# Hybrid streaming encoder step on one core: W_out loaded by parts, two output tiles under the last attention, scratch kept by token tile

## The chip, the cores and the metric

The kernel runs on one core of a Trainium2 chip. The metric is the device time of one execution in microseconds. The engines are named as in the profile: PE (TensorE, matmuls), DVE (VectorE), ACT (ScalarE), POOL (GpSimd) and SP (SyncE, whose queue issues all DMAs of this kernel).

## The reference, cut to what matters

One layer over 1024 prompt tokens and 8 x 16 sample tokens, 1152 in all, 1024 features wide. One projection gives the columns of three attention groups and a gate; the gated, concatenated attention outputs go through W_out, a residual and a LayerNorm.

```
h = x @ w_in                         # 3584 columns: A q,k,v; B q,k,v; M q; gate (1024)
o_a = band attention, 4 heads x 64, own chunk of 64 and 8 before, bias by distance
o_b = differential attention, 4 heads (2 maps of 64, values 128), rotary, then RMS norm and gain
o_m = attention of 4 heads x 64 into 256 memory tokens, keys and values from mem @ w_mem_kv
y = (concat(o_a, o_b, o_m) * silu(gate)) @ w_out
out = LayerNorm(ALPHA * x + y)       # and the new keys and values of each group are returned
```

The prompt attends to itself; each sample stream attends to its cache and its own 16 new tokens.

## The kernel before

All is fp32, and precision is kept by splitting: each operand becomes a rounded high part (fp32r) and the rest as a low part, and a product is three matmuls (high x high, high x low, low x high). A split is an ACT copy and a DVE or POOL subtraction (`split_half`, L122, for the input weights).

Tokens go in 3 chunks of 384 (`CH`) for the projections and in 9 tiles of 128 for the output. x lies split in SBUF all through the projections, in pool `xp`: `x{h,l}{c}`, 3 chunks of 8 feature rows. W_in has 28 blocks of 128 columns; a block is 3 chunks x 8 feature rows x 3 matmuls (`step`, L139). Two weight blocks are held (`wst`, tags `whi`, `wlo`), and `load_next` (L127) loads and splits the next one when a block begins, in the order of the list `order` (L113 to L119).

Heads go in pairs, as 8 units in the order `ORD` = M0, B0 to B3, A0, A1, M1. A unit has a key block, a value block, its attention over 8 query tiles, and the stages of its sample part. The attention (`attention_m`, `_b`, `_a`) is a list of steps with weights; `merge` (L943) mixes it with a filler list, the projections that don't depend on it: the unit's values, `NG[i]` gate blocks and the next unit's queries. Sample stages (`sample`, L774) are spread over later fillers (`with_stages`). Within this written order the planner places each instruction on its engine by a model of when its inputs are ready, so work may stand far ahead of where it is written.

A query tile's scores are two matmuls (L440, L441); DVE takes the row maximum (L588, L753, or with bias L701), ACT the exponential with its row sum, PE transposes it (L453), ACT and DVE split it (L456, L457), PE multiplies with the values (L627, L666). For A and M0 the sums are not divided out there: they are kept in `u.r`, and `finish` (L496) turns them into factors, written to the scratch `rscr`. For M1 (`slot == 7`) the rows are divided at once (`normalise`, L521), and its output stays in SBUF (`u.out`). For B the factor also holds the RMS norm.

Scratch in DRAM lies by column block: `oscr` [7, 128, 1152] takes the outputs of the seven other units, `gscr` [8, 128, 1152] the eight gates (L430), `rscr` [2, 8, 9, 128] the factors.

In the before kernel the last unit, M1, has two gate blocks as its filler. Behind it comes the output part. `mixed(t)` (L1032) loads for tile t the gates (L1037), the outputs (L1039) and, by six broadcasts over 64 partitions, the factors of A, B and M (L1044); it multiplies (L1048, L1058, L1062) and splits (L1054, L1055). W_out is loaded (L1149) and split (L1150, L1151) into the room of x, once the last gate has read x. Tiles 0 and 1 run k by k together, in four PSUM accumulators of two pools (`ps_s`, `ps_p`); tiles 2 to 8 run one after another in pieces of 512 columns (`piece`, L1097), with M1's sample stages between them. `add` (L1089) adds the residual (`xn`, loaded at L1076) and takes statistics, `norm` (L1103) normalises and stores. For tile 8 the second piece is cut in two of 256 columns, and the norm is shared between engines.

Cached keys and values of the samples go through one buffer (`sp`, tag `kc`). LayerNorm's scales are loaded behind W_out, `ln_g` into the buffer `tab0`, `ln_b` into `ka0`, which also holds the keys `u.ka[0]` of the attention.

## Time and profile before

| | |
|---|---|
| three runs | 698.63 us median (697.14 to 699.35) |
| profiled execution | 695.99 us, span 694.2 us |
| mean granted PE clock | 0.981 |
| busy: PE, DVE, ACT, POOL | 667.8, 467.1, 352.8, 210.3 us |
| DMA queue | 79.95 MB, 35.7% of 16 engines' span |

PE stands as busy over 96% of the span, but its matmuls are pipelined and their ends are modelled, so the share doesn't say how fast they follow each other; the distance from one start to the next does. `PEclk` is the share of the full clock (2.4 GHz) that was granted in a stretch; half speed is 1.2 GHz. In groups of instructions, "idle" is the time the engine stood before them and `<-` what released it. DMA times run from issue to landing.

### The profile page before, as it was taken

Reading aid. Unit: us, or ns where it says so; the run is one execution under the profiler, and the core shown is the slowest. Engines: PE = TensorE matmul, PEld = TensorE weight load, DVE = VectorE, ACT = ScalarE, POOL = GpSimd, SP = SyncE. Lnnn points to the kernel's source line nnn. Section 1 sums busy time; section 2 is a strip of 40 time slices with the busy share of each in tenths; the row PEclk is TensorE's granted clock in tenths of the full one; section 3 lists DMA queues with packets and bytes.
Section 4 is the critical chain, followed back from the end, with each engine's and each line's share of the span. In section 5 each row is a group of like instructions: output and inputs, shape, how many; then the busy total and the mean of one; then the engine's idle time right before and its main releaser. Section 6 shows DMA issues by size and latency. Waiting matters only on the chain.

```text
span 694.2 us, 12200 instructions
## 1 busy us (share of the span) xinstructions
PE 667.8 (96%) x4309; PEld 617.9 (89%) x4309; DVE 467.1 (67%) x1119; ACT 352.8 (51%) x917; POOL 210.3 (30%) x250
## 2 busy tenths in 40 slices
PE   8899999999999999999999999999999979798995
PEld 7799899999899999999999999999999958576784
DVE  4968756887687766896767256663566785788744
ACT  6748635575555645565557455574575762111000
POOL 7653213532343333432423121211110322223102
PEclk9999999999999999999999999999999979899998
DMA  8751432121212221152202121322232389897311
GB/s 280 255 197 58 143 116 74 50 94 70 66 50 83 83 89 61 50 172 92 75 24 90 69 73 51 108 73 96 92 108 88 122 243 280 237 272 222 117 66 61
DMA packets 68785, 80.72 MB, mean 116 GB/s; under 512 B 10210, under 2 KB 49780, under 8 KB 68724
## 3 DMA queue, kind: packets, MB, share of 16 engines
q1 hardware_dynamic: 68724, 79.95, 35.7%
q8 instruction: 34, 0.56, 0.3%
q14 instruction: 27, 0.22, 0.1%
HBM read 59.46 MB, written 20.46 MB: 115 GB/s over the span
## 4 chain that ended last, share of the span: by engine, by line
PE 82%; DMA 7%; DVE 5%; ACT 2%; issue 2%; SPq 2%; POOL 0%; POOLq 0%; DVEq 0%
PE pp L140 16%; PE pp L142 16%; PE pp L141 16%; PE ps L1087 5%; PE pt L453 5%; PE po L627 4%; PE ps L440 4%; PE ps L441 4%; PE pp L1087 4%; PE po L666 3%; DMA p<-gates 2%; PE pt L878 1%; SPq L1044 1%; PE ps L794 1%; DVE xl L198 1%
## 5 line engine op out<-in xcount | busy, mean ns | idle before, releaser
L140 PE MATMUL pp<-xh,whi 128*128 128x384 f32 x672 | 230.7, 344 | 1.1 <-DVE t L429 0.8
L141 PE MATMUL pp<-xl,whi 128*128 128x384 f32 x672 | 228.8, 341 | 2.4 <-DVE xl L198 1.8
L142 PE MATMUL pp<-xh,wlo 128*128 128x384 f32 x672 | 229.1, 341 | 0.0
L141 PEld LDWEIGHTS pp<-xl,whi 128*128 128x128 f32 x672 | 126.5, 188 | 6.0 <-DVE xl L198 2.4
L140 PEld LDWEIGHTS pp<-xh,whi 128*128 128x128 f32 x672 | 126.5, 188 | 4.6 <-DVE t L429 1.5
L142 PEld LDWEIGHTS pp<-xh,wlo 128*128 128x128 f32 x672 | 126.4, 188 | 1.8 <-issue 0.2
L125 POOL TENSOR_TENSOR wlo<-wraw,whi 128x512 fp32r<-128x512 f32 x54 | 73.0, 1372 | 144.0 <-ACT whi L124 142.0
L593 ACT ACTIVATE p<-ps,nm 128x512 f32<-128x512 f32 (+3 forms) x96 | 55.2, 580 | 56.5 <-DVE nm L590 37.7
L440 PE MATMUL ps<-ka,qa 128*128 128x512 f32 (+4 forms) x176 | 58.1, 337 | 1.2 <-ACT p L754 1.2
L441 PE MATMUL ps<-kl,qa 128*128 128x512 f32 (+4 forms) x176 | 56.8, 326 | 0.0
L453 PE MATMUL pt<-ident,p 128*128 128x128 f32 x332 | 55.0, 278 | 1.6 <-DVE rs L485 1.0
L588 DVE TENSOR_REDUCE nm<-ps 128x1 f32<-128x512 f32 (+3 forms) x96 | 50.9, 546 | 4.4 <-PE ps L441 2.8
L453 PEld LDWEIGHTS pt<-ident,p 128*128 128x128 f32 x332 | 40.3, 143 | 4.3 <-DVE rs L485 1.4
L457 DVE TENSOR_TENSOR ptl<-pt,pth 128x512 fp32r<-128x512 f32 x56 | 38.1, 684 | 5.7 <-ACT pth L456 5.4
L456 ACT CAST pth<-pt 128x512 fp32r<-128x512 f32 x56 | 32.4, 586 | 17.8 <-PE pt L453 11.0
L1054 ACT CAST whi<-p 128x1024 fp32r<-128x1024 f32 (+2 forms) x9 | 8.6, 954 | 62.6 <-PE pp L1087 39.1
L124 ACT CAST whi<-wraw 128x512 fp32r<-128x512 f32 x54 | 30.9, 620 | 9.9 <-PE pp L141 7.4
L440 PEld LDWEIGHTS ps<-ka,qa 128*128 128x128 f32 x176 | 33.1, 189 | 1.8 <-ACT p L754 1.4
L627 PE MATMUL po<-pth,va 128*128 128x256 f32 (+1 forms) x160 | 34.1, 284 | 0.0
L461 DVE TENSOR_TENSOR ptl<-pt,pth 128x256 fp32r<-128x256 f32 (+1 forms) x72 | 25.3, 352 | 13.1 <-ACT pth L460 12.7
L441 PEld LDWEIGHTS ps<-kl,qa 128*128 128x128 f32 x176 | 33.2, 189 | 0.2
L519 POOL COPY r<-rs 128x1 f32<-128x1 f32 x32 | 6.5, 203 | 88.4 <-DVE rs L597 44.7
(241 smaller groups left out, 1335.9 us busy)
## 6 DMA issues: line engine op xcount, KB each, us to landing
wraw<-in_win SPq DMA_DIRECT2D x54, 256.0 KB, 2.8
xr<-in_xT SPq DMA_DIRECT2D x12, 384.0 KB, 7.8
gates<-t SPq DMA_DIRECT2D x24, 192.0 KB, 1.9
qa<-in_xn SPq DMA_DIRECT2D x9, 512.0 KB, 6.1
out_y<-qa SPq DMA_DIRECT2D x16, 256.0 KB, 3.0
mixed<-od SPq DMA_DIRECT2D x28, 128.0 KB, 2.4
p<-mixed SPq DMA_DIRECT2D x8, 448.0 KB, 6.5
p<-gates SPq DMA_DIRECT2D x7, 512.0 KB
```

The costliest lines, as they stand in the source:

```text
L125: eng.tensor_tensor(out=lo[:, h], in0=raw, in1=f(hi[:, h]), op=ALU.subtract)
L140: nc.tensor.matmul(ps, lhsT=w[0][:, k], rhs=xh_[:, k], start=(k == 0), stop=False)
L141: nc.tensor.matmul(ps, lhsT=w[0][:, k], rhs=xl_[:, k], start=False, stop=False)
L142: nc.tensor.matmul(ps, lhsT=w[1][:, k], rhs=xh_[:, k], start=False, stop=(k == KT - 1))
L440: nc.tensor.matmul(ps, lhsT=u.qa[h][:, qs], rhs=u.ka[h][:, k0 : k0 + n], start=True, stop=False)
L441: nc.tensor.matmul(ps, lhsT=u.qa[h][:, qs], rhs=kl[h][:, k0 : k0 + n], start=False, stop=True)
L453: nc.tensor.transpose(pt[:, t, q * P : (q + 1) * P], p[q][:, cols[t][q] : cols[t][q] + P], ident)
L457: nc.vector.tensor_tensor(out=lo, in0=pt, in1=f(hi), op=ALU.subtract)
L588: nc.vector.tensor_reduce(out=nm[:, m, c : c + 1], in_=ps[c][:, : b - a], axis=AX.X, op=ALU.max, negate=True)
L593: nc.scalar.activation(e[:, a:b], ps[c][:, : b - a], AF.Exp, bias=nm[:, m, 0:1], accum_out=rs[:, m, c : c + 1])
L627: nc.tensor.matmul(out, lhsT=a, rhs=b, start=(g == 0 and x == 0), stop=(g == j and x == len(mm) - 1))
L1087: nc.tensor.matmul(y, lhsT=a[:, k], rhs=b[k][:, s], start=(k == 0 and x == 0), stop=(k == KT - 1 and x == 2))
```

## The change

- `NG` becomes [1, 1, 1, 1, 1, 1, 2, 0]: one gate runs at the start beside M0's query, chunk by chunk, and the last two run under A1 instead of M1. The second weight block is loaded ahead of x's chunks 1 and 2.
- Under A1, behind the queries of M1, the two gates run by chunk, and behind each chunk `load_wout(c)` loads up to three rows of W_out into that chunk's part of x.
- M1's filler is `out_steps(0)` and `out_steps(1)`: inputs, products by k, add and norm of the output tiles 0 and 1, both in `ps_p`. Row k = 7 (M1's own output) is handed out only when M1's pair of query tiles is closed; `merge` takes no more filler while it isn't.
- `normalise` divides all rows of A and M, samples too; `factors` and its scratch go, and `rscr` holds B's factors alone, in one broadcast per tile.
- The scratch lies by token tile: `oscr` [9, 128, 7, 128], `gscr` [9, 128, 8, 128]. A tile's load is one run per partition (3.5 or 4 KB instead of 7 or 8 runs of 512 bytes); a gate's store is three runs of 512 bytes per partition instead of one of 1.5 KB.
- The sample's matmuls get a priority, and M1's sample takes its key and value buffers from the pool `pp` (six buffers).

`add`, `products`, `piece` and `norm` are moved up unchanged but for the names of the scales.

```diff
-NG = [0, 1, 1, 1, 1, 1, 1, 2]
+NG = [1, 1, 1, 1, 1, 1, 2, 0]
...
-    oscr = dram.tile([7, P, NTOK], F32, tag="mixed")
-    gscr = dram.tile([8, P, NTOK], F32, tag="gates")
+    oscr = dram.tile([9, P, 7, P], F32, tag="mixed")
+    gscr = dram.tile([9, P, 8, P], F32, tag="gates")
...
-    rscr = dram.tile([2, 8, 9, P], F32, tag="rstd")
+    rscr = dram.tile([9, 4, P], F32, tag="rstd")
...
             for blk in range(4):
                 mem_part(blk)
+            load_next(ep)
             load_x(1)
             load_x(2)
-            load_next()
...
-            nc.sync.dma_start(gscr[slot, :, c * CH : (c + 1) * CH], t)
+            nc.sync.dma_start(
+                gscr[3 * c : 3 * c + 3, :, slot].rearrange("t p c -> p t c"), t.rearrange("p (t c) -> p t c", c=P))
...
-                nc.scalar.activation(
-                    e[:, :n], e[:, :n], AF.Exp, bias=nm, scale=-1.0, accum_out=u.r[:, 9 * h + i : 9 * h + i + 1])
+                rs = small.tile([P, 1], F32, tag="rs")
+                nc.scalar.activation(e[:, :n], e[:, :n], AF.Exp, bias=nm, scale=-1.0, accum_out=rs)
+                normalise(e[:, :n], rs, False)
...
-                    if u.slot == 7:
-                        normalise(e[:, h], u.r[:, 9 * h + i : 9 * h + i + 1], h == 1)
+                    rs = small.tile([P, 1], F32, tag="rs")
+                    nc.scalar.activation(e[:, h], ps, AF.Exp, bias=nm[:, h : h + 1], accum_out=rs)
+                    normalise(e[:, h], rs, h == 1)
...
-                               lambda: close_pair(u, st["po"], j))
+                               lambda: (close_pair(u, st["po"], j), closed.append(j)))
...
-            with tc.manual_schedule(engines={PE}):
+            with tc.high_priority(offset=SP_), tc.manual_schedule(engines={PE}):
...
+        def last(tag, shape):
+            return pp.tile(shape, F32, tag="p") if u.slot == 7 else sp.tile(shape, F32, tag=tag)
...
             while fill and done_f < lead + (total_f - lead) * rate * done_m / total_m:
-                c, g = fill.pop(0)
+                if len(fill[0]) == 3 and not fill[0][2]():
+                    break
+                c, g = fill.pop(0)[:2]
...
+    def mixed(t):
+        ts_ = slice(t * P, (t + 1) * P)
+        gt = sp.tile([P, KT, P], F32, tag="kc") if t == 0 else pp.tile([P, KT, P], F32, tag="p")
+        nc.sync.dma_start(gt, gscr[t])
+        mx = op_.tile([P, 7, P], F32, tag="tab0") if t == 0 else pp.tile([P, 7, P], F32, tag="p")
+        nc.sync.dma_start(mx, oscr[t])
+        rs = tmp.tile([P, 4, P], F32, tag="rs", bufs=2)
+        nc.sync.dma_start(rs, rscr[t].rearrange("(o k) c -> o k c", o=1).broadcast_to([P, 4, P]))
+        nc.vector.scalar_tensor_tensor(
+            out=mx[:, 2:6], in0=mx[:, 2:6], scalar=subg, in1=rs, op0=ALU.mult, op1=ALU.mult)
+        mh, ml = [wst.tile([P, KT, P], F32R, tag=tag) for tag in ("whi", "wlo")]
...
+        (nc.vector if t < 2 else nc.gpsimd).tensor_tensor(out=gt[:, 0:7], in0=mx, in1=gt[:, 0:7], op=ALU.mult)
+
+        def last():
+            nc.vector.tensor_tensor(out=gt[:, 7], in0=units[7].out[:, ts_], in1=gt[:, 7], op=ALU.mult)
+            parts(slice(7, 8) if t < 2 else slice(0, 8))
+
+        if t < 2:
+            parts(slice(0, 7))
+        else:
+            last()
+        return mh, ml, last
...
+    def load_wout(c):
+        room = [xp.tile([P, 3, 1024], F32R, tag=f"x{i}{c}") for i in "hl"]
+        for k in range(3 * c, min(3 * c + 3, KT)):
+            hi, lo = woh[k], wol[k] = [r[:, k - 3 * c] for r in room]
+            for n in range(2):
+                s = slice(512 * n, 512 * n + 512)
+                raw = wst.tile([P, 512], F32, tag="wraw")
+                nc.sync.dma_start(raw, d["wout"][k, :, s])
+                nc.scalar.copy(hi[:, s], raw)
+                (nc.gpsimd if n else nc.vector).tensor_tensor(out=lo[:, s], in0=raw, in1=f(hi[:, s]), op=ALU.subtract)
+
+    def out_steps(t, u):
+        st = {}
+        def go(k):
+            if k == 0:
+                start(t)
+                if t == 0:
+                    scales()
+                st["y"] = [ps_p.tile([P, 512], F32, tag="pp") for _ in CUTS]
+            if k == KT - 1:
+                outs[t].m[2]()
+            for cut, y in zip(CUTS, st["y"]):
+                products(t, cut, y, k)
+            if k == KT - 1:
+                residual(t)
+                for n, (cut, y) in enumerate(zip(CUTS, st["y"])):
+                    add(t, n, cut, y)
+                norm(t)
+        steps = [(1.4, lambda k=k: go(k)) for k in range(KT - 1)]
+        return steps + [(1.4, lambda: go(KT - 1), lambda: t // 2 in u.closed)]
+
+    def scales():
+        for w, tag in (("ln_g", "tab0"), ("ln_b", "ka0")):
+            norms.append(op_.tile([P, 1024], F32, tag=tag))
+            nc.sync.dma_start(norms[-1], d[w].broadcast_to([P, 1024]))
...
             if i == 6:
-                stages = sample_of(u)[:-1]
+                for c in range(3):
+                    for g in gs:
+                        fill += g[c]
+                    fill.append((0.0, lambda c=c: load_wout(c)))
+                stages = sample_of(u)
...
-            fill = more
+            fill = out_steps(0, u) + out_steps(1, u)
```

## Rows read from the trace of the kernel before

**Rows 1.** Stretches: busy us of PE, PEld, DVE, ACT, POOL; clock; DMA; GB/s

```profile
480.00:540.00 60.00, 60.00 (x441) 58.58 (x440) 36.21 (x108) 36.08 (x97) 6.00 (x8) 1.00 0.26 87
540.00:560.00 20.00, 16.46 (x108) 15.19 (x107) 15.12 (x41) 15.30 (x42) 5.73 (x4) 0.97 0.45 145
560.00:580.00 20.00, 18.83 (x85) 15.52 (x84) 18.16 (x35) 11.78 (x22) 6.20 (x4) 0.77 0.93 283
580.00:600.00 20.00, 15.90 (x82) 12.24 (x80) 8.81 (x18) 2.68 (x3) 4.21 (x2) 0.91 0.85 231
600.00:620.00 20.00, 20.00 (x92) 15.48 (x92) 17.23 (x28) 2.07 (x5) 6.64 (x4) 0.92 0.98 277
620.00:640.00 20.00, 17.39 (x106) 13.47 (x104) 16.60 (x33) 2.76 (x6) 6.17 (x4) 1.00 0.79 233
640.00:660.00 20.00, 19.92 (x109) 15.99 (x110) 15.59 (x27) 1.31 (x2) 3.93 (x3) 0.91 0.36 132
660.00:680.00 20.00, 20.00 (x87) 16.09 (x86) 11.21 (x19) 1.05 (x1) 1.83 (x2) 1.00 0.15 56
```

**Rows 2.** The chain that ended last, its last matmuls: start us, us, what

```profile
652.64 5.62 PE ps L1087 x24
...
680.75 5.65 PE pp L1087 x48
```

**Rows 3.** Stretch 540 to 694, L1087 alone: busy us of PE, PEld; clock; DMA

```profile
540.00:694.00 154.00, 109.11 (x456) 85.32 (x456) 0.92 0.60 183
```

**Rows 4.** Waits of PE, 500 to 694: us in total, times, longest

```profile
PE pt L878 <- DMA kc<-in_cmv: 2.7, 1, 2.7
PE ps L794 <- DVE qa L1094: 2.5, 1, 2.5
```

**Rows 5.** Timeline of PE: start us, us, instruction, idle before and its releaser

```profile
549.65 0.22 PE L666 MATMUL po<-ptl,va 128*64 128x128 f32 x1
...
582.66 0.28 PE L666 MATMUL po<-pth,va 128*128 128x256 f32 x1
...
598.29 1.22 PE L1087 MATMUL pp<-xh,whi 128*128 128x512 f32 x2 [1.60 <-DVE qa L1094]
```

**Rows 6.** Groups of splits on ACT, POOL and DVE: busy us, mean ns, idle

```profile
L124 ACT CAST whi<-wraw 128x512 fp32r<-128x512 f32 x54 | 30.9, 620 | 9.9 <-PE pp L141 7.4 <-issue 2.1 <-DMA wraw<-in_win 0.3
L125 POOL TENSOR_TENSOR wlo<-wraw,whi 128x512 fp32r<-128x512 f32 x54 | 73.0, 1372 | 144.0 <-ACT whi L124 142.0 <-DMA rs<-rstd 1.3 <-POOL qa L155 0.7
L1151 DVE TENSOR_TENSOR xl<-wraw,xh 128x512 fp32r<-128x512 f32 x2 | 2.1, 1052 | 0.4 <-ACT xh L1150 0.4
```

**Rows 7.** DMA issues: count, KB, median us to landing; then line L1044's

```profile
wraw<-in_win SPq DMA_DIRECT2D x54, 256.0 KB, 2.8
qa<-in_xn SPq DMA_DIRECT2D x9, 512.0 KB, 6.1
p<-mixed SPq DMA_DIRECT2D x8, 448.0 KB, 6.5
...
L1044 SPq DMA_DIRECT2D rs<-rstd x54: 512/599/3516, 396.3 to 633.9; - x54
```

**Rows 8.** Groups of DVE

```profile
L523 DVE RECIPROCAL ra<-ra 128x1 f32<-128x1 f32 x18 | 2.6, 152 | 0.9 <-ACT p L754 0.8
L528 DVE TENSOR_SCALAR p<-p,ra 128x256 f32<-128x256 f32 x8 | 3.1, 383 | 0.3
L921 DVE TENSOR_SCALAR tab<-tab 128x1280 f32<-128x1280 f32 x2 | 1.7, 849 | 0.3 <-DMA tab<-in_abias 0.3
L1094 DVE SCALAR_TENSOR_TENSOR qa<-qa,ps 128x512 f32<-128x512 f32 x9 | 6.0, 681 | 1.4 <-PE ps L1087 1.1
```

**Rows 9.** The first 30 us, and PE's largest hole in them

```profile
0.00:30.00 30.00, 25.12 (x154) 22.39 (x154) 19.26 (x23) 19.99 (x34) 22.93 (x28) 1.00 0.79 269
...
27.47 0.44 PE L141 MATMUL pp<-xl,whi 128*128 128x384 f32 x1 [1.64 <-DVE xl L198]
```

**Rows 10.** Timeline of SP's queue, W_out's first load

```profile
515.66 0.33 SPq L1149 DMA_DIRECT2D wraw<-in_wout  x1
```

More of the change, by code (lines that the diff above doesn't have):

```diff
@@ L24 @@
 BIG = 1e30
+SP_ = 100
 HP = 300
@@ L116, in hybrid_step @@
         order += [b + idx for b in base[kind][1:]]
-        order += [20 + next(gates) for _ in range(NG[i])]
+        late = [20 + next(gates) for _ in range(NG[i])]
+        if i != 6:
+            order += late
         if i < 7:
             order.append(base[names[i + 1][0]][0] + names[i + 1][1])
+        if i == 6:
+            order += late
     loaded = {}
@@ L496, in finish @@
     def finish(u):
-        src = u.ms if u.kind == "B" else u.r
-        if u.kind == "B":
-            factors_b(u)
-        else:
-            factors(u)
-        n = src.shape[-1]
-        pt = ps_t.tile([n, P], F32, tag="pt")
-        nc.tensor.transpose(pt, src, ident)
-        row = tmp.tile([n, P], F32, tag="od128", bufs=1)
+        factors_b(u)
+        pt = ps_t.tile([9, P], F32, tag="pt")
+        nc.tensor.transpose(pt, u.ms, ident)
+        row = tmp.tile([9, P], F32, tag="od128", bufs=1)
         nc.scalar.copy(row, pt)
-        for h in range(2):
-            nc.sync.dma_start(rscr[h, u.slot], row[n - 9 : n] if h else row[0:9])
+        nc.sync.dma_start(rscr[:, u.idx], row)
     def combine(u, ex, rs, n, t):
@@ L668, in attention_a @@
     def attention_a(u, need):
-        u.r = small.tile([P, 18], F32, tag="ra", bufs=2)
         blocks = []
@@ L739, in attention_m @@
             u.out = op_.tile([P, NTOK], F32, tag="tab1")
-        u.r = small.tile([P, 18], F32, tag="ra", bufs=2)
+        u.closed = closed = []
         blocks = []
@@ L907, in sample @@
             return stages
[L908 removed]
+        return stages
     def load_mem(u):
@@ L935, in emit @@
     def emit(items):
-        for _, fn in items:
-            fn()
+        for x in items:
+            x[1]()
     def stage():
@@ L945, in merge @@
         total_m = sum(w for w, _ in main)
-        total_f = sum(w for w, _ in fill)
+        total_f = sum(x[0] for x in fill)
         done_m = done_f = 0.0
@@ L1152, in hybrid_step @@
-    residual(0)
-    residual(1)
-    lng = op_.tile([P, 1024], F32, tag="tab0")
-    lnb = op_.tile([P, 1024], F32, tag="ka0")
-    nc.sync.dma_start(lng, d["ln_g"].broadcast_to([P, 1024]))
-    nc.sync.dma_start(lnb, d["ln_b"].broadcast_to([P, 1024]))
-    tn = [(t, n) for t in range(2) for n in range(2)]
-    ys = [ps_s.tile([P, 512], F32, tag="ps") if t == 0 else ps_p.tile([P, 512], F32, tag="pp") for t, n in tn]
-    for k in range(KT):
-        for (t, n), y in zip(tn, ys):
-            products(t, CUTS[n], y, k)
@@ new lines, in hybrid_step, with need @@
+    norms = []
+    def scales():
+        for w, tag in (("ln_g", "tab0"), ("ln_b", "ka0")):
+            norms.append(op_.tile([P, 1024], F32, tag=tag))
+            nc.sync.dma_start(norms[-1], d[w].broadcast_to([P, 1024]))
+    stages = []
+    late = []
+    first = [q_of(units[0])] + [gate_block(next(gates)) for _ in range(NG[0])]
+    for parts in zip(*first):
+        for part in parts:
+            emit(part)
+    for i, u in enumerate(units):
+        nxt = units[i + 1] if i + 1 < len(units) else None
+        emit(with_stages(sum(k_of(u), []), EV))
+        if u.kind != "M":
+            while stages:
+                stage()
+            flush_tiny()
+        if u.kind == "B":
+            vb, ve = v_block(u, 14 + u.idx, o["bvT"][u.idx], 0)
+        elif u.kind == "A":
+            tables_a(u)
+            vb, ve = v_block(u, 4 + u.idx, o["avT"][u.idx], 512)
+        else:
+            vb, ve = [], []
+        more = []
+        gs = [gate_block(next(gates)) for _ in range(NG[i] if i else 0)]
+        if i != 6:
+            more += sum(sum(gs, []), [])
+        if nxt:
+            more += sum(q_of(nxt), [])
+            fill = vb + more[:4] + ve + more[4:]
+            if i == 6:
+                for c in range(3):
[3 more added lines that the diff above has]
+                stages = sample_of(u)
+                fill = fill[:ES] + with_stages(fill[ES:], EV)
+            if u.kind == "M":
+                fill = with_stages(fill, 8)
+        else:
+            fill = out_steps(0, u) + out_steps(1, u)
+        def need(kt, u=u, fill=fill):
+            while u.vdone <= kt // 3:
+                fill.pop(0)[1]()
+        main = {"M": lambda: attention_m(u), "B": lambda: attention_b(u, need), "A": lambda: attention_a(u, need)}[u.kind]()
+        merge(main, fill, LEAD if u.kind != "M" else 1.0, RR if nxt else RL)
+        if i != 6:
+            ended = late[:]
+            late.clear()
+            now = sample_of(u)
+            stages = stages + now[:LW] + ended + now[LW:]
+        else:
+            while stages:
+                stage()
+            flush_tiny()
```

125 lines of the change are left out of this document (13 added, 112 removed).

## The prediction

> **What bounds the kernel now.** I read the profile in this order: the table of stretches, PE's waits, the chain of waits, then the groups of single engines.
>
> The table of stretches [rows 1] splits the run in two. From 480 to 540 us PE is busy all the time at full clock. From 540 to 640 us it is not: its busy times there are 16.46, 18.83, 15.90, 20.00 and 17.39 of 20 us, so 11.4 us are idle, and the granted clock falls to 0.97, 0.77, 0.91 and 0.92. It is 0.91 once more in 640 to 660. These are means of 2.4 and 1.2 GHz: (0.03 + 0.23 + 0.09 + 0.08 + 0.09) x 20 = 10.4 us of full clock are lost. In the same stretches DVE has 15 to 18 us of 20 in four of the five, and the DMA engines go from 0.26 to 0.45, 0.93, 0.85 and 0.98.
>
> The same loss can be counted. In the chain's end [rows 2] 24 matmuls of 512 columns take 5.62 us, 0.234 us each, and 48 of 256 columns 5.65 us, 0.118 each: 0.46 ns per column. After 540 us PE issues 456 products of L1087 [rows 3] (408 of 512 columns, 48 of 256: 95.5 + 5.7 = 101.2 us), the last 53 projections of 384 columns (0.176 each: 9.3) and what is left of the attention, some 100 transposes and products of 128 and 256 columns (10) and the sample's small ones (3), 123.5 us in all. The last matmul ends at 686.4 [rows 2], 146.4 us after 540. So 23 us of the last 146 are loss: 11.4 idle, and slow clock, some of whose 10.4 us fell on idle time, with short pauses for the rest. Behind the last matmul stand 7.8 us of a closing chain (686.4 to 694.2), which the change leaves alone.
>
> PE's waits name where the idle time comes from: 2.7 us for cached values that arrive late (L878 [rows 4]), 2.5 and 1.6 us for the residual add L1094 [rows 4, 5] (one event, and the two matmuls behind it take 1.22 us, where two of the closing chain take 0.47), and the other 4.6 us in small pieces, most of them inside M1's attention, which has too little beside it while ACT and DVE also split W_out. M1's last product stands at 582.66, A1's last, the 128-column one, at 549.65 [rows 5].
>
> **The change part by part.** PE's amount of work stays: the same 28 blocks, 456 products, the same attention. So the sum is about loss.
>
> (1) W_out moves. Its 16 loads of 256 KB and their splits, now spread up to the end of M1's scores and past it, go into A1's attention, as each part of x is released by the last two gates. What comes in there: ACT 16 x 0.62 = 9.9 us, DVE 8 x 1.05 at most, POOL 8 x 1.4 = 11 [rows 6]. In 480 to 540 ACT has 36.1 of 60 us, DVE 36.2, POOL 6.0 and DMA 0.26 [rows 1], and that stage gets a gate block more (12.6 us) to stretch over. Cost there: nothing; if ACT's cover were gone, at most the 3 to 4 us by which one part's splits can hold up the next. I take 0.
>
> (2) Output tiles 0 and 1 are M1's filler, in place of two gates. Their 2 x 11.2 = 22.5 us of products need, for each k, one split row of W_out, and for k = 7 M1's first pair. Rows 0 to 5 of W_out are free to load 8.4 us or more before the last gate ends (2 x 24 x 0.176), so tile 0 can run as soon as M1 starts. Its other inputs wait for A1's last score (it takes tab0), well ahead.
>
> (3) SP's queue. Per tile six L1044 issues of about 0.6 us [rows 7] become one: 3 us per tile, 27 in all, in a queue where other DMAs stand behind them. Two scratch loads per tile, 512 and 448 KB, land after 6.5 us, with runs of 512 bytes; they become runs of 4 and 3.5 KB. The residual, already in 4 KB runs, takes 6.1 [rows 7], so I give the layout itself nothing. What frees the DMA engines is that 4.2 MB of W_out and 192 of the 448 KB of broadcast per tile are gone from this stage. Gate stores go from 1.5 KB to 512-byte runs, 24 times, where the DMA engines have three quarters of their time free.
>
> (4) The sums are divided early. A0 and A1: 32 score rows, each a reciprocal (0.15 us) and one DVE scaling; the 128x256 one takes 0.38, a 128x1280 one 0.85 [rows 8], so some 0.3 to 0.5 by width: 19 us on DVE over two stages, and 0.6 us more from score to transpose. DVE is some 54 to 60% busy there and PE is 100% covered by projections. I take +1 us, bounded by 0 and by 32 x 0.6 = 19 if the cover failed every time; the row nearest is PE busy 60.00 of 60 [rows 1]. M0 pays 16 such rows under B0's query projection. Given back: the A and M passes of L1048, two per tile, off the path, and three tiny transposes.
>
> (5) The start. One gate is computed chunk by chunk with the first query. PE's largest hole there is 1.64 us [rows 9], some 2.6 with the smaller ones; a gate chunk has 4.2 us of matmuls to put into them. Against it: 512 KB of weights go ahead of x (1.9 us at 269 GB/s [rows 9]), and the third weight block must wait until the first is used up, with only one gate chunk and M0's scores (32 x 0.118 = 3.8 us) to hide its 2.8 us DMA and its splits of 0.62 and 1.37 us twice [rows 6, 7]. I take 0, ends -2.6 and +3.
>
> (6) The cached keys and values of M1's sample get their own buffers from a pool of six instead of one: the 2.7 us wait of L878 goes.
>
> What is late next in the M1 stage: DVE. It is busy 33.3 us in 540 to 580 [rows 1]. Without W_out (8 splits, 8 us at most) some 25 remain, and tiles 0 and 1 add four L1094 of 0.68 [rows 8] and four passes of statistics, which I take to be as long (5.4): 30 us, against 22.5 us of tile products and some 8 of M1's own matmuls. That is hardly covered; the two norms can trail, because the later tiles leave DVE 8.8 of 20 us (660 to 680, [rows 1]). I leave 7 us of the 23: one wait of the size of 2.5 + 1.6 between tile 0 and tile 1, whose four accumulators now share two PSUM buffers, the 2 us of slow clock that follow such a wait, and 1 for the rest.
>
> **Sum.** -16 (loss of 540 to 686), +1 (A0, A1), 0 (start), 0 (W_out): -15. The profiled execution took 695.99 us (span 694.2 and 1.8 around it), 2.6 below the median 698.63 of the three runs; on its scale 681.0, on the median's **683.6**. With the bounds above: -22 to -9, 676 to 690.
>
> **The rivals.**
> A. M1's own chain sets the stage. From A1's last product to M1's last it takes 33 us now [rows 5]; the matmuls to put beside it are 30.5. If half of the idle time of 540 to 600 (8.8 us) and half of its slow clock (7 us) stay on top of my 7: 8 us more, 691.6. For it: DVE at 18.2 of 20 in 560 to 580. Against: a fifth of that was W_out, and tile 2's products can follow as filler.
> B. The PSUM hand-over is dearer. Both buffers of tile 0 wait for M1's pair and the residual; tile 1 can't start before. The 4.1 us of [rows 4, 5] a second time and the slow clock after it: 6 us more, 689.6. The Trainium skill, "Perfetto Trace Analysis", section on matmuls, asks for independent groups to rotate through PSUM banks so that eviction lies under the next group; the kernel before, with four banks for the two tiles, does, and the wait of 4.1 us is still there, so the trace backs it only in part.
> C. All of it goes: 2 us of loss left, the start's holes filled: -20.7 - 2.6 = 675.3.
> D. Slower. ln_b now takes ka0, the buffer of M1's keys, and is asked for at tile 0's start. If SP holds that DMA until M1's last score, and the residuals and tile 2's inputs stand behind it, tile 0's adds wait, both PSUM buffers stay taken, and M1 runs without filler: 11.2 us of tile 1 uncovered, some 5 of slow clock, 5 to 6 for tile 2's late loads, and the 16 not won: 683.6 + 22 = 705.6. It decides from the point where ln_b stands ahead of the two residual loads. For it: SP issues one DMA after another, and that is the written order. Against: the planner orders issues by when they are ready: W_out's first load stands at 515.66, written behind all of M1 [rows 10].
> E. The division shows in A0 and A1 after all, at half of its 19 us: 692.
> That the change doesn't do what it says (tile 0's last step is held back until M1's first pair closes, and the filler stops there): it lies between A and B.
>
> **How the numbers follow.** Forecast 0.48, A 0.14, B 0.11, C 0.11, D 0.11, E 0.05. A measurement of this kernel tells about 0.3% (2.1 us) from no change: faster is below 696.5. Faster: forecast, A but for 0.03, B, C and E but for 0.01: 0.85; same 0.04; slower D, 0.11. The range 674 to 695 takes in the forecast's own 676 to 690, C, B and most of A and E, and leaves D out.
>
> **What would show it.** PE busy 18.5 us or more of each 20 from the start of M1 to the last matmul, and a clock of 1.00 but for one dip; no wait for in_cmv; W_out loads beside A1's products; nine L1044 issues; L1048 of 512 columns alone; the last matmul near 671 us on the profile. If M1's last product stands over 33 us behind A1's, or the clock has two or more dips, A or B holds; a load of ln_b ahead of the residuals with PE idle behind it shows D. I would be wrong if A0 and A1 grew idle PE time, or if the first 60 us lost more than 3 us.

## The result, and the profile after

The changed kernel takes 702.39 us (median of 5 runs, 701.83 to 704.89), the kernel before 697.70 beside it (5 runs, 696.85 to 699.35): ratio 1.0074, 95% interval 1.0049 to 1.0099. It is slower, and outside the predicted range; the forecast was 683.6. The profiled execution took 702.39 us, its span 700.6.

The stretches of the changed kernel, columns as in [rows 1]:

```profile
540.00:560.00 20.00, 14.54 (x66) 12.04 (x65) 15.40 (x42) 13.62 (x35) 5.10 (x4) 0.74 0.57 181
560.00:580.00 20.00, 17.58 (x111) 14.78 (x110) 10.62 (x31) 10.16 (x28) 0.00 (x0) 1.00 0.02 7
580.00:600.00 20.00, 13.08 (x53) 9.64 (x52) 15.12 (x40) 8.49 (x23) 0.92 (x1) 0.74 0.70 251
600.00:620.00 20.00, 18.45 (x110) 14.39 (x109) 11.27 (x22) 4.29 (x8) 6.15 (x3) 1.00 0.70 244
620.00:640.00 20.00, 20.00 (x148) 15.97 (x147) 18.85 (x29) 3.14 (x7) 8.26 (x6) 1.00 0.73 249
```

From 600 us on it went nearly as predicted: PE is busy 18.45 and 20.00 of 20 us at clock 1.00, where [rows 1] have a clock of 0.92 in the first of these stretches and 17.39 us in the second. But 540 to 560 and 580 to 600 are worse than anything before: PE 14.54 and 13.08 of 20, the clock at 0.74 in both. Between them DMA stands still (0.02), in the very stretch in which tile 1's inputs should come.

To compare kernels I use one figure, the loss: the distance from each matmul's start to the next one's, less 0.457 ns per column (the pace of [rows 2]), summed over a stretch, without the sample's small matmuls. It holds idle time, slow clock and pauses too short to count as idle. Each row is one profiled execution, and these lie up to 3.3 us off their kernel's median (before 695.99 against 698.63, e5 686.68 against 683.75):

| loss, us | 0-60 | 60-440 | 440-540 | 540-560 | 560-580 | 580-600 | 600 on | from 540 |
|---|---|---|---|---|---|---|---|---|
| before | 11.5 | 24.3 | 8.4 | 6.0 | 6.1 | 5.2 | 6.4 | 23.7 |
| changed | 12.3 | 23.4 | 6.5 | 11.9 | 5.7 | 12.3 | 2.2 | 32.1 |
| small parts alone (e5) | 13.3 | 22.9 | 7.8 | 8.1 | 5.7 | 0.2 | 0.7 | 14.7 |
| e18 | 12.2 | 23.4 | 6.5 | 12.3 | 4.7 | 4.9 | 0.5 | 22.4 |
| e19 | 12.6 | 23.9 | 11.6 | 1.9 | 7.0 | 1.5 | 0.7 | 11.1 |

And these are the events of the stage, from the timelines (us; A1's last score is the end of the last DVE pass that adds A1's bias, the other events are starts):

| | A1's last score | M1's row maxima | last projection | tile 0's first product | tile 1's first product | M1's last pair closed | last matmul |
|---|---|---|---|---|---|---|---|
| before | 518.3 | 518.9 to 559.6 | 553.6 | 564.9 | with tile 0 | 584 | 686.1 |
| changed | 543.2 | 548.4 to 588.1 | 543.3 | 554.8 | 593.0 | 618 | 692.4 |
| e5 | 519.8 | 519.9 to 564.7 | 550.4 | 566.1 | with tile 0 | 599 | 676.7 |
| e12 | 543.4 | 546.8 to 588.9 | 544.2 | 556.2 | 593.1 | 609 | 690.8 |
| e17 | 544.0 | 550.8 to 593.8 | 544.8 | 558.5 | 585.3 | 607 | 691.1 |
| e18 | 541.5 | 548.3 to 577.2 | 542.7 | 555.9 | 585.3 | 603 | 682.6 |
| e19 | 536.0 | 554.8 to 577.7 | 551.0 | 551.6 | 579.5 | 602 | 677.1 |

The two gates more in front of A1's last score (one at the start, one under A1) move it from 518 to 543, and M1 behind it by 29 us. The projections now end with that score, where they went on for 35 us before. PE's largest waits in the changed kernel (line waited for: us in total, times, longest), against [rows 4]:

```profile
PE ps L448 <- ACT p L752: 4.1, 2, 3.6
PE pp L1031 <- ACT whi L995: 3.1, 2, 2.1
PE po L663 <- ACT pth L468: 2.8, 3, 1.8
PE pp L146 <- DVE qa L163: 2.5, 1, 2.5
```

The wait for in_cmv is gone, as predicted. L1031 is `products`, L995 the split of a tile's inputs. PE's timeline in the changed kernel has both of those waits and the long one for M1's exponentials:

```profile
554.80 0.80 PE L1031 MATMUL pp<-xh,whi 128*128 128x512 f32 x1 [1.04 <-ACT whi L995]
...
585.65 0.39 PE L448 MATMUL ps<-ka,qa 128*128 128x256 f32 x1 [3.62 <-ACT p L752]
...
592.97 0.80 PE L1031 MATMUL pp<-xh,whi 128*128 128x512 f32 x1 [2.06 <-ACT whi L995]
```

The first line is tile 0's first product, 11.5 us behind the last projection; the third is tile 1's, 11 us behind tile 0's last. SP's queue in the changed kernel shows why the loads were late (start, us, issue):

```profile
544.09 0.42 SPq L987 DMA_DIRECT2D tab<-mixed  x1
...
554.29 0.33 SPq L1084 DMA_DIRECT2D wraw<-in_wout  x1
555.01 21.02 SPq L442 DMA_DIRECT2D mixed<-od  x2
583.30 0.34 SPq L1020 DMA_DIRECT2D qa<-in_xn  x1
583.74 0.38 SPq L985 DMA_DIRECT2D p<-gates  x1
584.22 0.37 SPq L987 DMA_DIRECT2D p<-mixed  x1
586.52 0.33 SPq L1116 DMA_DIRECT2D ka<-in_ln_b  x1
```

Tile 0's outputs are loaded at 544.09, into the buffer of A1's bias table, right behind A1's last score. Then SP stands for 20 us at the store of A1's last pair, and for 7 more at tile 1's residual; tile 1's gates and outputs stand behind. Of the 10.7 us from tile 0's load to its first product, 4.8 go by until DVE's first pass over it; the other 5.9 go to the passes and the split, which take their turn between M1's own work. Two rows of DVE's timeline and one of ACT's:

```profile
548.91 0.74 DVE L990 SCALAR_TENSOR_TENSOR tab<-tab,subg,rs 128x512 f32<-128x512 f32 x1
...
551.44 1.08 DVE L998 TENSOR_TENSOR kc<-tab,kc 128x896 f32<-128x896 f32 x1
...
553.81 0.94 ACT L995 CAST whi<-kc 128x896 fp32r<-128x896 f32 x1
```

SP's waits in 550 to 592 name the releasers, A1's last close and tile 0's add:

```profile
SPq L442 <- DVE od L648: 20.6, 2, 20.3
SPq L1020 <- DVE qa L1038: 7.2, 1, 7.2
```

DVE in the changed kernel, at the end of tile 0:

```profile
581.99 1.29 DVE L1038 SCALAR_TENSOR_TENSOR qa<-qa,pp 128x512 f32<-128x512 f32 x2
583.19 1.28 DVE L1039 BATCH_NORM_STATS2 st<-qa 128x6 f32<-128x512 f32 x2
...
584.63 1.03 DVE L750 TENSOR_REDUCE nm<-ps 128x1 f32<-128x256 f32 x3
...
588.46 0.28 DVE L1001 TENSOR_TENSOR p<-tab,p 128x128 f32<-128x128 f32 x1
...
589.87 0.75 DVE L990 SCALAR_TENSOR_TENSOR p<-p,subg,rs 128x512 f32<-128x512 f32 x1 [0.79 <-DMA p<-mixed]
```

The three row maxima of M1 (L750), and three more after them, stand in DVE's order behind tile 0's add and statistics, and tile 1's passes (L1001, L990) behind those. So there are two suspects for the hole of 580 to 600, SP's order and DVE's order, and one for that of 540 to 560, A1's last score.

The DMA issues, for [rows 7]: one broadcast per tile, and the tile loads land in half the time.

```profile
qa<-in_xn SPq DMA_DIRECT2D x9, 512.0 KB, 3.5
wraw<-in_wout SPq DMA_DIRECT2D x16, 256.0 KB, 4.4
p<-mixed SPq DMA_DIRECT2D x8, 448.0 KB, 3.4
rs<-rstd SPq DMA_DIRECT2D x9, 256.0 KB, 3.9
```

### The profile page after: what moved, and what is told of

The parts are those of the page before. It is cut to its first block, busy times and chain, and to the rows that moved or that the text cites. A ratio compares the mean times of both kernels' runs of the same rounds, so it can differ in the third digit from the quotient of the medians.

```text
span 700.6 us, 12139 instructions
## 1 busy us (share of the span) xinstructions
PE 669.1 (96%) x4306; PEld 620.0 (88%) x4306; DVE 483.8 (69%) x1201; ACT 354.0 (51%) x922; POOL 211.9 (30%) x250
## 4 chain that ended last, share of the span: by engine, by line
PE 83%; DMA 5%; DVE 5%; ACT 3%; POOL 1%; issue 1%; SPq 0%; POOLq 0%; ACTq 0%; DVEq 0%
PE pp L146 16%; PE pp L147 16%; PE pp L148 16%; PE pp L1031 7%; PE ps L1031 6%; PE pt L461 4%; PE po L624 4%; PE ps L449 4%; PE ps L448 4%; PE po L663 3%; DMA wraw<-in_wout 2%; DVE xl L204 1%; PE pt L875 1%; DMA p<-mixed 1%; PE ps L790 1%
## 5 line engine op out<-in xcount | busy, mean ns | idle before, releaser
L131 POOL TENSOR_TENSOR wlo<-wraw,whi 128x512 fp32r<-128x512 f32 x52 | 70.5, 1376 | 110.7 <-ACT whi L130 104.0
L1031 PE MATMUL pp<-xh,whi 128*128 128x512 f32 (+1 forms) x96 | 38.0, 395 | 3.1 <-ACT whi L995 3.1
L1031 PE MATMUL pp<-xl,whi 128*128 128x512 f32 (+1 forms) x96 | 37.3, 388 | 0.0
L1031 PE MATMUL pp<-xh,wlo 128*128 128x512 f32 (+1 forms) x96 | 36.4, 385 | 0.0
L161 POOL TENSOR_TENSOR qa<-t,qa 64x384 fp32r<-64x384 f32 (+1 forms) x24 | 22.0, 918 | 38.1 <-ACT qa L159 37.1
```

Source lines behind the costliest of these rows:

```text
L131: eng.tensor_tensor(out=lo[:, h], in0=raw, in1=f(hi[:, h]), op=ALU.subtract)
L1031: nc.tensor.matmul(y, lhsT=a[:, k], rhs=b[k][:, s], start=(k == 0 and x == 0), stop=(k == KT - 1 and x == 2))
```

## The experiments

Times are medians; each ratio is to runs of the kernel before on the same chip (its medians 698.55 to 699.11), with its 95% interval. The edits start from the changed kernel unless said otherwise.

### The small parts without the moves: e5, p3, p4, p6

e5 has the schedule of the kernel before, with the rest of the change:

```diff
-NG = [1, 1, 1, 1, 1, 1, 2, 0]
+NG = [0, 1, 1, 1, 1, 1, 1, 2]
-            load_next(ep)
             load_x(1)
             load_x(2)
+            load_next()
-            fill = out_steps(0, u) + out_steps(1, u)
+            fill = more
...
+    # W_out, tiles 0 and 1 behind M1 with four accumulators, as in the kernel before
```

> The schedule of the kernel before (gates 0,1,1,1,1,1,1,2, W_out loaded after the last gate, tiles 0 and 1 together in four accumulators after M1) with the small parts of the change alone: scratch by token tile, sums divided early, one broadcast of B's factors per tile, own buffers for M1's sample. Theory T7 (these parts are a gain, the moves are the loss): the waits for in_cmv and the crowded DMA of 560 to 620 go, 694 to 696. Rival (the early division costs in M0, A0 and A1): loss in 400 to 520 grows by 3 us or more, 698 to 701.

683.75 us, ratio 0.9795 (0.9769 to 0.9821): better than T7 hoped for, and almost to the digit, by luck, what I had forecast for the whole change. So the small parts win 14.3 us (2.05% of 698.6), and the moves lose 19.5 again (1.0074 against 0.9795). Its stretches:

```profile
540.00:560.00 20.00, 15.83 (x93) 14.82 (x92) 16.21 (x36) 14.02 (x38) 6.90 (x5) 0.85 0.65 206
560.00:580.00 20.00, 17.58 (x90) 14.87 (x89) 14.84 (x37) 12.31 (x31) 4.25 (x4) 0.89 0.46 160
580.00:600.00 20.00, 20.00 (x124) 16.08 (x123) 17.80 (x31) 5.23 (x10) 5.19 (x3) 1.00 0.91 331
600.00:620.00 20.00, 20.00 (x148) 16.00 (x147) 18.31 (x29) 2.47 (x9) 9.28 (x5) 1.00 0.77 265
```

PE is full from 580 on, with both tiles behind M1 and W_out still loaded there. Then each part alone, on the kernel before:

```diff
 # p3: layout by token tile
-oscr[u.slot, :, a:b]
+oscr[a // P : b // P, :, u.slot].rearrange("t p c -> p t c")     # gscr, loads alike
 # p4: sums divided early, factors of B alone
+normalise(e[:, :n], rs, False)
+nc.sync.dma_start(rs, rscr[t].rearrange("(o k) c -> o k c", o=1).broadcast_to([P, 4, P]))
 # p6: M1's sample
-kc = sp.tile([P, 2, 4, P], F32, tag="kc")
+kc = pp.tile([P, 2, 4, P], F32, tag="p")                         # vc alike, and SP_
```

> The kernel before with the scratch by token tile alone (same number of DMAs, longer runs in the tile loads). My prediction gave the layout nothing: 698 to 699. Rival (the 512-byte runs are what fills the DMA queues in 560 to 620): DMA share there falls from 0.9 to 0.6, W_out and the residuals land earlier, 690 to 693.

694.14 us, 0.9930 (0.9904 to 0.9957). My "nothing" was wrong; the rival was right in kind, though less came of it, and DMA's share in 600 to 620 only fell from 0.98 to 0.91. What fell is the number of packets. The DMA summary of 560 to 680, of the kernel before, then of p3, then of e5:

```profile
DMA packets 28512, 24.24 MB, mean 202 GB/s; under 512 B 1593, under 2 KB 24249, under 8 KB 28502
```

```profile
DMA packets 16562, 25.25 MB, mean 210 GB/s; under 512 B 1670, under 2 KB 9896, under 8 KB 16552
```

```profile
DMA packets 8056, 21.47 MB, mean 179 GB/s; under 512 B 880, under 2 KB 1136, under 8 KB 8048
```

The layout takes out 14,000 of 24,000 packets below 2 KB, the one broadcast most of the rest. How the time follows from the packets, the landing times don't show: a residual load, which the layout doesn't touch, goes from 6.1 us [rows 7] to 5.6 in p3, but W_out's loads into `wraw` go from 3.8 to 4.7. (In the changed kernel, where W_out and most of the broadcast are gone from the stage too, the residual takes 3.5.) The Trainium skill, "Perfetto Trace Analysis", section DMA Optimizations, says that transfers under 2 KB carry a significant overhead each, and that larger ones are the main thing to try where HBM is much used and DMA is the limit. I had read the equal landing times of [rows 7] as a sign that the layout doesn't matter; p3's 4.9 us, in a stage where the DMA share is 0.79 to 0.98, agree with the page.

> The kernel before with the sums of A and M0 divided early, and with that one broadcast of B's factors per tile instead of six of all. My prediction: +1 us for the division and no more than some 3 us from the shorter SP queue: 697 to 699. Rival (the six broadcasts of 448 KB and their issues are what makes the end of the kernel wait): 690 to 692, with the waits for the residual add gone.

691.70 us, 0.9894 (0.9871 to 0.9916): the rival. The waits of PE for the residual add (2.5 and 1.6 us in [rows 4, 5]) are no longer among its eight largest, and the loss of 440 to 540 is 7.9 us against 8.4: the division under A0 and A1 costs nothing that shows. Where the gain comes from is not shown. p4 takes away several things at once: five issues and 192 of 448 KB of broadcast per tile, two DVE passes per tile, and packets (21,164 are left in 560 to 680, while the residual still lands after 6.2 us). Of the 4.0 us between the two profiled executions about half falls after 540 (loss 21.7 us against 23.7).

> The kernel before with the own buffers and the priority of M1's sample alone. My prediction: the wait of 2.7 us for in_cmv goes, 696; with the layout (-4.9) and the division with one broadcast (-7.3) that gives the -14.8 of the three together. Rival (the load only waits for SP and DMA in the crowd, not for its buffer): the wait stays, 698 to 699.

697.45 us, 0.9982 (0.9960 to 1.0003). The wait for in_cmv goes, but another takes part of its place (3.7 us for a tile's split). Not told from no change. The three ratios multiplied give 0.9807, e5 measured 0.9795: the parts add up.

### Who holds SP's queue: e1, e2, e6, e7, e8, e12

```diff
 # e1
-nc.sync.dma_start(oscr...)                       # keep
+(nc.scalar if u.slot == 1 else nc.sync).dma_start(oscr...)
 # e2: mixed(0)
-mx = op_.tile([P, 7, P], F32, tag="tab0") if t == 0 else ...
+mx = pp.tile([P, 7, P], F32, tag="p")
 # e6: split_mem
-u.ka = [op_.tile([P, 256], F32R, tag=f"ka{i}") for i in range(2)]
+u.ka = units[6].ka if u.slot == 7 else ...
```

> A1's five stores of its outputs are issued by ACT instead of SP, so nothing in SP's queue stands behind the close of A1's last pair. Theory T1 (in the changed kernel SP stands 20 us at that store, 555 to 575, and tile 1's inputs and the residuals behind it start at 583): tile 1's first product moves from 593 to 580 or earlier, the DMA share of 560 to 580 rises from 0.02 to over 0.2, the loss in 580 to 600 goes from 12 us to some 5: 5 to 7 us faster than the changed kernel, 696 us. Theory T2 (the stage is late because tile 0's inputs and M1's keys wait for A1's last score at 543): the first product of tile 0 stays at 554.8, 540 to 560 still loses 12 us, and M1's own chain sets 580 to 600 too: less than 2 us.

702.37 us, 1.0039 (1.0018 to 1.0060). Tile 1's residual and inputs now wait by themselves, 580.57 and 580.99 instead of 583.30 and 583.74; DMA in 560 to 580 stays at 0.02. T1 as I put it is refuted: the 20 us at A1's store hid a second wait, that of tile 1's residual for tile 0's add. SP's wait in e1:

```profile
SPq L1020 <- DVE qa L1038: 27.1, 1, 27.1
```

> Tile 0's attention outputs are loaded into a buffer of the pool of six, not into the buffer that holds A1's bias table until A1's last score. T2: the load stands before 544, tile 0's first product before 552 instead of 554.8, 540 to 560 loses 3 to 5 us less, time 698 to 700. T1: the hole of 580 to 600 stays as it is (tile 1's first product still behind the 20 us hold of SP); what tile 0 wins is lost again there: 702, no change.

702.33 us, 1.0047 (1.0021 to 1.0072); tile 0's first product stays at 555.2. But the load hardly moved: in e2's order it stands behind that of `ln_g`, which now took the bias table's buffer, and it left SP at 543.29 instead of 544.09 and landed 5.6 us later. So this run doesn't tell what an early load would give; it shows that another buffer alone doesn't make it early.

```profile
542.22 0.42 SPq L1116 DMA_DIRECT2D tab<-in_ln_g  x1
...
543.29 0.38 SPq L987 DMA_DIRECT2D p<-mixed  x1
```

> M1's keys (256 columns) go into the first 256 columns of A1's own key tiles, so they wait only for the scores that read these columns (query tiles 0 to 5), not for A1's last score. T2: M1's first row maximum moves from 548 to 540 or earlier, M1's pairs close some 5 to 8 us earlier, 540 to 560 loses 4 to 6 us less, time 696 to 699. T1 alone: the pairs close earlier, but tile 1 still waits for SP: 1 to 2 us at most.

705.19 us, 1.0092 (1.0064 to 1.0121): M1's first row maximum came at 550.9, not earlier. Another order, no gain; that M1's keys wait for A1's last score is not shown to cost anything.

```diff
 # e7
-u.xn = op_.tile([P, 1024], F32, tag="qa0", bufs=2)
+u.xn = op_.tile([P, 1024], F32, tag="qa1" if t == 1 else "qa0", bufs=2)
-u.z = op_.tile([P, 1024], F32, tag="qa1", bufs=2)
+u.z = u.xn if t < 2 else op_.tile([P, 1024], F32, tag="qa1", bufs=2)
-("ln_b", "ka0")
+("ln_b", "kc")
 # e8 = e7 + e1;  e12 = e8 with ln_b in "ka1" and M1's keys together in "ka0"
```

> The residual of tile 1 no longer goes into the buffer of M1's queries (free only after M1's last score) but into A1's other query buffer, where the sum is then formed in place for tiles 0 and 1; ln_b goes into the sample's buffer instead of that of M1's keys. A1's stores stay on SP. Theory T5 (what holds tile 1's inputs in SP's queue until 581 to 583 is the residual of tile 1, waiting for M1's last score; the hold at A1's store only hides it): SP is free when A1's last pair closes, 575; tile 1's inputs are asked for there instead of 583.7, its first product stands at 583 to 586 instead of 593; 580 to 600 loses 5 us less: 696 to 698. Theory T6 (DVE has tile 0's add, statistics and norm in its order ahead of M1's last row maxima and of tile 1's inputs): the loads come early, but the first product stays at 588 or later: 700 to 702.

699.26 us, 1.0017 (0.9997 to 1.0036), tile 1's first product at 590.9: T6's sign, at a little less than T6's time. Tile 1's gates went out at 578.59, 5 us earlier; behind A1's store ln_b now stood at the head of SP's queue for 4.5 us. (The text above says that the residual waited for M1's last score. The trace says otherwise: it had tile 0's residual buffer and waited for tile 0's add, L1038.)

> The same, and A1's stores are issued by ACT: nothing in SP's queue waits between 554 and the end of tile 0. T5: tile 1's inputs land by 565, its first product follows tile 0's last by less than 4 us (both PSUM buffers have to be emptied), near 582; DMA share of 560 to 580 over 0.15; 7 to 9 us faster than the changed kernel: 693 to 695. T6: as above, under 2 us.

699.92 us, 1.0024 (1.0004 to 1.0043). Now ln_b stood at the head of SP's queue, for 22.2 us, until tile 0's gates were used up; tile 1's inputs still went out at 579.67.

> As the run with the residual and A1's stores moved, but ln_b goes into the second key buffer (M1's two key tiles, 256 columns each, share the first), which is free after A1's last score. In the run before, ln_b stood in SP's queue until tile 0's gates were used up (579) and tile 1's inputs still behind it. Now nothing in SP's queue waits on M1. T5: tile 1's inputs are asked for before 560 and its first product follows tile 0's last by under 4 us, near 582: 693 to 695. T6 (the six last row maxima of M1 and tile 1's inputs stand in DVE's order behind tile 0's add, statistics and norm): first product at 588 or later, 698 to 700.

700.62 us, 1.0020 (1.0004 to 1.0036). Tile 1's inputs go out at 574 (what holds them now is the ring of six buffers that they share with M1's rows), 10 us earlier than in the changed kernel, and its first product stands at 593.1 as there, as T6 says. SP's issue and DVE's row in e12 (lines are one higher here):

```profile
574.09 0.33 SPq L986 DMA_DIRECT2D p<-gates  x1
```

```profile
581.78 1.28 DVE L1039 SCALAR_TENSOR_TENSOR qa<-qa,pp 128x512 f32<-128x512 f32 x2
...
584.42 1.03 DVE L751 TENSOR_REDUCE nm<-ps 128x1 f32<-128x256 f32 x3
...
590.04 0.74 DVE L991 SCALAR_TENSOR_TENSOR p<-p,subg,rs 128x512 f32<-128x512 f32 x1
```

L991, tile 1's first large pass, waits for nothing but its turn: DVE has been busy without a pause since 580.90. All SP repairs together are worth 2 to 4 us.

### DVE's order and tile 1's inputs: e13, e17, e18

```diff
 # e13 = e12 and
-RL = 0.95
+RL = 0.5
 # e17 = e12 with ln_b in "kc" again and, in mixed(1)
+gt = op_.tile([P, KT, P], F32, tag="ka1")
+mx = op_.tile([P, 7, P], F32, tag="qa1", bufs=2)
 # e18 = e17 with RL = 0.5
```

> The same, and the filler under M1 is handed out at half the rate (RL 0.5 instead of 0.95), which puts all 16 row maxima of M1 ahead of tile 0's add in DVE's order. T6: the PE wait of 3.6 us for M1's exponentials goes, M1's last pair closes near 590 instead of 607 to 619, tile 1 follows tile 0 at once; 540 to 620 loses 8 to 12 us less than in the changed kernel: 688 to 692. If M1's chain (A rival: too little beside it) is what limits, the loss only moves: 697 to 700.

697.39 us, 0.9980 (0.9965 to 0.9995): the wait of 3.6 us is gone, M1's last pair closes at 598, but tile 1's gates are asked for at 580.11 and its first product stands at 590.5: the inputs are still late. The order is mended here, the queue is not: tile 2's residual, which needs M1's last score, stands ahead of them in SP's queue.

```profile
SPq L1021 <- PE ps L450: 16.0, 1, 16.0
```

> Tile 1's gates and outputs go into A1's second key buffer and A1's second query buffer, both free after A1's last score, so they are asked for near 543 and are multiplied and split before M1's last scores; ln_b goes into the sample's buffer behind them; A1's stores on ACT. If late inputs of tile 1 are the cause: tile 1's first product follows tile 0's last within 3 us (582 instead of 593), 580 to 600 loses 4 us instead of 12: 692 to 694. If M1's scores behind tile 0's add, or too little work beside M1, is the cause: tile 1 runs early, but PE idles later, while M1's last pairs close: 697 to 700.

699.09 us, 1.0014 (0.9995 to 1.0032). Tile 1 follows tile 0 at once, and the hole comes back behind it, while M1's last pairs close:

```profile
585.27 0.50 PE L1032 MATMUL pp<-xh,whi 128*128 128x512 f32 x1 [0.75 <-DVE qa L1039]
```

```profile
580.00:600.00 20.00, 18.07 (x95) 14.48 (x92) 16.24 (x43) 8.55 (x25) 0.92 (x1) 1.00 0.41 155
600.00:620.00 20.00, 14.31 (x80) 10.60 (x81) 15.19 (x27) 4.68 (x9) 6.94 (x4) 0.83 0.83 295
```

> The same with RL 0.5, so that M1's 16 row maxima stand ahead of tile 0's add on DVE. If inputs and DVE's order together are the cause: M1 and both tiles end by 605, loss of 540 to 620 falls from 31 us to 14 (as in the kernel with the small parts alone): 686 to 688. If the late start of M1 is the cause: A1's tail (543 to 556) still loses 11 us, since no tile can start before A1's last score, and the total stays at 692 to 695.

694.29 us, 0.9937 (0.9912 to 0.9962). With inputs and order both mended the hole of 580 to 600 falls from 12.3 to 4.9 us of loss, and 600 on is clean. Against the changed kernel e17 gains 3 us, e13 5 and e18 8 (by the ratios 4, 7 and 10). But all three also hold SP's repairs: early inputs alone (e17 against e8) are worth 0.8 us, not told from none, the order alone (e13 against e12) 3.2, and both together (e18 against e8) 5.6. What is left is 540 to 560, 12.3 us. The second branch of the expectation holds in the total: in this schedule nothing is there to be put beside A1's end.

### The gate at the start: e4, e9, e19, e21, e22

```diff
 # e4;  e9 = e8 + this;  e19 = e18 + this
-NG = [1, 1, 1, 1, 1, 1, 2, 0]
+NG = [0, 1, 1, 1, 1, 2, 2, 0]
-            load_next(ep)
             load_x(1)
             load_x(2)
+            load_next()
 # e21 = e5 with a gate at the start, second weights ahead of x
+NG = [1, 1, 1, 1, 1, 0, 1, 2]
 # e22 = e19 with
+NG = [0, 1, 1, 1, 2, 1, 2, 0]
```

> The gate that runs beside M0's query goes under A0 instead (NG 0,1,1,1,1,2,2,0), and the second weight block is loaded behind x again, as before the change. Theory T4 (the start cost 1.5 us and the offset is carried): loss in 0 to 40 falls from 12.1 to 10.5 us, the rest is unchanged: 701 us. If the stretched A0 pushes A1's scores later still, 540 to 600 does not get better and the time stays at 701 to 703.

698.33 us, 0.9995 (0.9973 to 1.0017): the first place, 0 to 60, gains nothing, but 540 to 560 loses 4.9 us instead of 11.9. Part of that is paid ahead of it: 440 to 540 loses 13.4 us instead of 6.5, 8.1 of it in 460 to 500, behind A0's last scores.

> The same as the last, and no gate at the start (it runs under A0). T4 and T5 add up if the start's 4 us (measured alone: 698.3 against 702.4) and the hold of SP are separate: 689 to 691. If both only pay the same hole in 540 to 600: 694.

694.64 us, 0.9950 (0.9935 to 0.9965): 5 us below e8, as e4 is 4 below the changed kernel. The time is that of the second branch, but both branches took SP's repair to be worth 7 to 9 us; with the 2.5 that e8 measured, the two add up.

> The same without the gate at the start (under A0 instead). The two pairs measured so far say 4 to 5 us less than the run before this one: 687 to 690; the loss of 540 to 560 falls from 11 to 2 us, because the projections then reach past A1's last score.

687.08 us, 0.9846 (0.9818 to 0.9873). The projections go on to 551, tile 0 starts 0.6 us behind them. The loss of 540 to 560 falls by 10.4 us, that of 440 to 540 grows by 5.1. The stretches of e18, then of e19:

```profile
540.00:560.00 20.00, 13.46 (x72) 11.36 (x71) 16.39 (x40) 11.09 (x28) 4.30 (x3) 0.74 0.76 244
560.00:580.00 20.00, 17.63 (x112) 15.09 (x110) 14.59 (x49) 15.55 (x46) 1.28 (x1) 1.00 0.18 54
```

```profile
540.00:560.00 20.00, 19.40 (x123) 17.98 (x122) 14.75 (x32) 11.00 (x26) 4.40 (x3) 1.00 0.77 236
560.00:580.00 20.00, 16.57 (x95) 12.98 (x95) 15.42 (x54) 16.57 (x47) 3.84 (x3) 1.00 0.32 99
```

> The kernel with the small parts alone, but A0's gate is computed at the start beside M0's query and the second weight block is loaded ahead of x. If the gate at the start costs by itself (M0's query must wait for its weights): 1.5 us or more in 0 to 40, 685 to 686. If what it cost in the moved schedule was only where the projections ended (beside A1's tail), it costs nothing here: 683 to 684.

687.24 us, 0.9831 (0.9803 to 0.9858), 3.5 us above e5, more than either branch said. Its loss from 540 on is small (9.5), that of 440 to 540 large (13.9 against 7.8, 9.7 of it in 460 to 500). That is where A0 ends, which gave up its gate; that its end is bare for this reason is not shown.

> As the run with tile 1's inputs early, RL 0.5 and no gate at the start, but the gate of the start goes under B3 (NG 0,1,1,1,2,1,2,0) instead of A0. If the start itself costs (M0's query beside a gate, second weights ahead of x): 687 as with A0. If what counts is that A0 is drawn out, so that the last projections reach past A1's last score: they end with it again (543), 540 to 560 loses 11 to 12 us, 693 to 694.

689.17 us, 0.9864 (0.9835 to 0.9893): neither branch. A0 is not drawn out, and the projections still end at 549.6, 10 us behind A1's last score (539.3), with 2.1 us of loss in 540 to 560. So in the moved schedule they end together in every run with a gate at the start, and in none of the four without one, whichever unit gets the gate (the second weight block went behind x with it each time); why the planner places the last gates so differently stays open.

The best kernel measured is e5, 683.75 us; it beats both the kernel before and the changed one. The moved schedule with all repairs (e19) comes to 687.08. Its profiled execution loses less from 540 on than e5's (11.1 against 14.7 us) and as much more in 440 to 540 (11.6 against 7.8); but e5's profiled execution, 686.68, lies 2.9 us above its median, so where the 3.3 us between the medians lie stays open.

## Why the prediction was wrong, point by point

The step that failed is (2). Its sentence "so tile 0 can run as soon as M1 starts. Its other inputs wait for A1's last score (it takes tab0), well ahead" took A1's last score from the old schedule, 35 us ahead of the last projection [in the table above]. In the new one the gates that (1) puts under A1, and the one of (5), draw A1's scores out to 543.2, level with the last projection; tile 0's inputs are loaded at 544.09, and its first product stands at 554.8. The filler that M1 lost, two gates, needed no input. The filler it got needs A1's end, its own loads, multiplications and splits, and for k = 7 M1's first pair. Measured: the loss of 540 to 600 is 29.9 us instead of 17.3. In the sum it is the term -16 that failed: the loss from 540 on was to fall by 16 us, and it grew from 23.7 to 32.1. That the missing cover is the cause of the hole in 540 to 560, e4, e9 and e19 show: where projections reach past A1's last score, it loses 1.9 to 4.9 us instead of 11.9, though tile 0 starts no earlier behind that score. Of the 18.6 us between e5 and the changed kernel, e18's repairs give back 8.1 and the gate taken from the start 7.2 more, net of what it costs ahead of 540; the last 3.3 stay open.

(1) "Cost there: nothing" was right inside A1 (loss of 440 to 540: 6.5 against 8.4; W_out's loads stood at 508.4 to 554.3, beside A1), and wrong by what the longer stage moves: M1's row maxima start 29 us later. No run moves W_out alone; e19, which still moves it, comes within 3.3 us of e5, which doesn't.

(2), tile 1: I counted its 11.2 us of products as work beside M1. They started when M1's last maxima were done. Two causes, each hidden behind the other: late inputs and M1's last scores behind tile 0's add on DVE. With SP's repairs below them, early inputs gave 3.3 us against the changed kernel (e17), the order 5.0 (e13), both 8.1 (e18).

(3) The term was missing from the sum: the layout gave 4.9 us where I took 0 (p3). The early division with one broadcast gave 7.4 (p4), where I counted 3 us per tile of issue time as room, gave it no term of its own, and took +1 for the division; p4 doesn't separate the two, nor the queue from the bytes.

(4) +1 us: a cost of the division shows nowhere. (6) -2.7: the wait goes, the gain is -1.3, within 0.3% of none.

(5) 0 with the end at +3: 3.5 to 7 us (e21, e4, e9, e19), and not in the first 60 us (12.3 against 11.5). In the moved schedule it costs through where the last projections end; in e5's schedule (e21) it costs in 460 to 500.

"What is late next" named DVE and the hand-over between tile 0 and tile 1, and left 7 us. In e18 PE waits 2.29 us at the hand-over by its timeline, less than the 4.1 I allowed; in the changed kernel DVE was the limit by its order, not by its load (10.62 and 15.12 of 20 us in 560 to 600).

The sum, -15, agrees with e5's -14.3, but that is luck: I drew it from hiding M1's holes with tiles 0 and 1, which e5 doesn't do. There it came from parts to which I gave next to nothing: 4.9 us from the layout, 7.4 from the early division with one broadcast, 1.3, not told from none, from the sample's buffers.

The rivals: A had the sign of what happened, M1's chain with too little beside it, at 691.6 far too cheap; "33 us against 30.5 of matmuls" assumed all 30.5 to be ready. D was the slower one, and a load that isn't ready at the head of SP's queue did stand ahead of tile 1's inputs in the changed kernel; but there it was A1's store and tile 1's residual (ln_b only after my repairs, in e7 and e8), and it decided 2 to 4 us, not 22. B and E were not seen. The listed signs were the right ones: two dips of the clock, M1's last product more than 33 us behind A1's.

## What to carry to other kernels

Before moving filler from one stage to another, ask when its inputs are there in the new schedule, not in the old: work that needs nothing (a projection) is worth more beside a dependent chain than work that needs the chain's predecessor, and moving it ahead also moves the chain. When a load looks late, free the buffer behind the one that the trace names too, and read the order of the engine that consumes it: here every repair of the queue only found the next holder. And change schedule and plumbing separately: the small parts alone were worth 14 us, and the moves hid it.

## What the runs showed of the hardware

I had not expected the length of runs to matter where the DMA engines move 200 to 300 GB/s anyway: from 560 to 680 us, 28,512 packets against 16,562 for nearly the same bytes (24.24 and 25.25 MB) went with 4.9 us (0.9930). The landing times of loads that were not touched don't explain it (a residual 6.1 and 5.6 us, W_out's loads into `wraw` 3.8 and 4.7, before and in p3). A hole was paid for about twice: in the changed kernel's two bad stretches PE is idle for 5.5 and 6.9 us, the granted clock (a mean of 1.2 and 2.4 GHz) is 0.74 in both, and the loss is 11.9 and 12.3 us. The slow clock isn't all of that: between them, in 560 to 580, PE is idle for 2.4 us at clock 1.00, and the loss is 5.7.
